# Packed small operands, a new order of the first loads and an earlier split of the first input weights in a two-block transformer kernel

## The chip, the core and the metric

One core of a Trainium2 chip runs the whole program. The metric is the device time of one execution in microseconds; three runs of the kernel before have a median of 1456.27 us (1455.43 to 1457.64). The engines are named as in the profile: PE (TensorE matmul), PEld (its weight load), DVE (VectorE), ACT (ScalarE), POOL (GpSimd) and SP (SyncE, which here issues the DMAs; its queue is SPq).

## What is computed

A batch of one sequence of 256 tokens, width 1024, float32, passes through two blocks. The part that matters here is the first:

```python
mod = jax.nn.silu(c) @ w_ada[l] + b_ada[l]            # 1024 x 6144
sh1, sc1, gt1, sh2, sc2, gt2 = jnp.split(mod, 6, axis=-1)
h = modulate(rmsnorm(x, g_norm1[l]), sh1, sc1)
y = hybrid_mixer(h, w_in[l], ...)
x = x + gt1[:, None, :] * y
h = modulate(rmsnorm(x, g_norm2[l]), sh2, sc2)
y = hierarchical_moe(h, w_rg, b_rg, w_re, b_re, w_e_gate, w_e_up, w_e_down)   # 32 experts, 2 per token
x = x + gt2[:, None, :] * y
# hybrid_mixer
z = h @ w_in
glu_a, glu_b, q, k, v, o, i_pre, f_pre, g_a, g_b = jnp.split(z, offs, axis=-1)
u = jax.nn.silu(layernorm(causal_dwconv(glu_a * sigmoid(glu_b), conv_dw_w, conv_dw_b), ...))
y_a = u @ w_conv_out
hm = mlstm_chunkwise(q, k, v, i_g, f_g)               # 4 heads, then a norm per head, times sigmoid(o)
y_b = hm @ w_m_out
merged = sigmoid(g_a) * y_a + sigmoid(g_b) * y_b
```

The second block has two layers, each with a modulation of the same kind (`ada_w_2`), attention and a gated feed-forward part.

## The kernel before, in words

**Weights.** `load` (L65) takes one of 8 buffers `raw` of 1 MB and has SP issue one DMA into it; there are some 400 MB of weights, so this stream runs through the whole program. A weight that meets a matrix is split in two float32r halves: ACT copies it into `hi`, DVE subtracts to get `lo` (`split` L92, `split_cols` L108 and L110), and `mm3` issues three matmuls (L119 to L121: lo by Hh, hi by Hl, hi by Hh). The activations are split in the same way into `Hh` and `Hl`.

**The modulation.** `mod` is made from `w_ada` in groups of steps (`ada_steps`): each step loads one 1 MB slab and issues 4 matmuls of fp32 into one bank `ada` (the profile counts 8 for the 4); the second step of a block's group first adds the bias by 4 more. The last copies the bank to `adarow` (ACT, L227). Then a use step follows: `ada_cols` (4 matmuls `adac`) and `mod_cols` (DVE, tile `AB`), or `ada_gate`, which splits `adarow` (`gtmp`; ACT copy, DVE subtraction L115), spreads it with 4 matmuls `adag` and copies the two banks to `gate`. The first group (`ada0`, eight steps and a use step) runs at the start; the other three groups of the block stand in the list `queue`, and `fill()` takes the next step from it, one after each input slab, so that their loads and matmuls lie between the others. `fill(len(queue))` before the output products of the mixer takes what is left, and then the steps of the second block's first layer (`cc2`, `ada_w_2`) are appended.

**The start.** SP issues `cs` (constants, 435 KB), small vectors into rows of `vrow`, then the eight slabs of `w_ada` with up to three small loads of the list `late` behind each, x behind the fourth, the second part of the constants `ca`, the gate weights `wif`, the biases `bif` and `brt`, the router weights `wr`, and only then the first slab of `w_in`. Three PE transposes turn `vrow` and `wdr` into columns (`vct`, `wdct`), which DVE and ACT read. x is normed and transposed into four banks `nt` (two halves of the columns by two halves of the tokens), `norm_post` applies the modulation (ACT L344 and DVE L342, tile `gtmp`) and splits the result into `Hh` (L351) and `Hl` (L115). Then `first()` takes each slab of `w_in`: split, 48 matmuls, `fill()`. Four slabs give `glua`, `glub`, `glua`, `glub`, then come the slabs of q and k, the gates, v, the mLSTM in four steps (`pS`, `pw`, `num`), `ga` and `gb`; the normed `hm` is transposed (`hmT`) in between.

**The layer norm of the convolution.** DVE runs the convolution beside the matmuls (`uacc`, L621 and L624). At its end come 4 matmuls `lnm` (mean), ACT's copy, DVE's subtraction (L633), ACT's square (L635), 4 matmuls `lnv`, ACT's root (L640), DVE's reciprocal (L641) and product (L642). The output products `yb` (from `hmT`) and `ya` (from `uacc`) follow.

The order on each engine is set by the tile framework from this program text; an engine runs its instructions in that order.

Of the kernel before, what the change touches and what calls it, by code (L numbers as in the profile page):

```python
# [7 lines left out]
F32 = mybir.dt.float32  # L8
# [3 lines left out]
AF = mybir.ActivationFunctionType  # L12
# [6 lines left out]
KT = 8  # L19
# [9 lines left out]
C_P = 870  # L29
# [8 lines left out]
V_C, V_C2, V_GN1, V_CB, V_LG, V_LB, V_QB, V_GN2 = 0, 8, 16, 24, 28, 32, 36, 44  # L38
V_N1, V_N2, V_MG, V_SG, V_QW, V_LAM, V_END = 52, 68, 84, 88, 89, 121, 125


@with_exitstack
def kernel(ctx: ExitStack, tc: tile.TileContext, I, cst, out):
# [12 lines left out]
    def pb(name):  # L56
        return psum.tile([128, 512], F32, name=name, tag="pb", bufs=3)
# [14 lines left out]
    def load_k(w, k0, k, n0, n):  # L72
        return load(w[k0 * 128:(k0 + k) * 128, n0:n0 + n].rearrange("(k p) n -> p k n", p=128), k, n)
# [54 lines left out]
    early = pha.enter_context(tc.tile_pool(name="early", bufs=1))  # L128
    vrow = early.tile([128, 128], F32, name="vrow")
    x = act.tile([128, 2, D], F32, name="x")  # L130
    wdr = early.tile([124, 128], F32, name="wdr")
    bif = const.tile([8, 1], F32, name="bif")
    brt = const.tile([128, 36], F32, name="brt")
    wr = const.tile([128, KT, 36], F32, name="wr")

    POOL.memset(vrow, 0.0)

    def vload(nm, off, n):
        SP.dma_start(out=vrow[off:off + n], in_=I[nm].rearrange("o (n p) -> (o n) p", p=128))
# [3 lines left out]
    vload("c_2", V_C2, 8)
    vload("g_norm1", V_GN1, 8)
    def lload(i, nm):
        SP.dma_start(out=vrow[V_LAM + i:V_LAM + i + 1, 0:64], in_=I[nm])

    late = [lambda: ada_bias(0, I["b_ada"][0]),
            lambda: vload("conv_dw_b", V_CB, 4), lambda: vload("conv_ln_g", V_LG, 4),
            lambda: vload("conv_ln_b", V_LB, 4), lambda: vload("qk_conv_b", V_QB, 8),  # L150
            lambda: vload("g_norm2", V_GN2, 8), lambda: vload("norm1_g_2", V_N1, 16),
            lambda: vload("norm2_g_2", V_N2, 16), lambda: vload("m_norm_g", V_MG, 4),
            lambda: vload("a_subln_g_2", V_SG, 1),
            lambda: lload(0, "a_lam_q1_2"), lambda: lload(1, "a_lam_k1_2"),
            lambda: lload(2, "a_lam_q2_2"), lambda: lload(3, "a_lam_k2_2"),
            lambda: SP.dma_start(out=vrow[V_QW:V_QW + 32], in_=I["qk_conv_w"].rearrange("o w (n p) -> (o w n) p", p=128)),
            lambda: SP.dma_start(out=wdr, in_=I["conv_dw_w"].rearrange("o w (n p) -> (o w n) p", p=128))]

# [15 lines left out]
    selrr = const.tile([128, 128], F32R, name="selrr")  # L174
    DVE.tensor_copy(selrr, selr)
    half = const.tile([128, 1], F32, name="half")
    POOL.memset(half, -0.5)

    vc = const.tile([128, V_END], F32, name="vc")
    pt = pb("vct")  # L180
    PE.transpose(pt[:, 0:8], vrow[0:8], ident[0:8, 0:8])
    cc = const.tile([128, 8], F32, name="cc")
    ACT.activation(cc, pt[:, 0:8], AF.Silu)
    cc2 = const.tile([128, 8], F32, name="cc2")

# [213 lines left out]
    pt = pb("vct")
    PE.transpose(pt[:, 0:V_END], vrow[0:V_END], ident[0:V_END, 0:V_END])  # L400
    DVE.tensor_copy(vc, pt[:, 0:V_END])
    ACT.activation(cc2, vc[:, V_C2:V_C2 + 8], AF.Silu)
# [18 lines left out]
    wif = pp.tile([128, KT, 8], F32, name="wif")
    SP.dma_start(out=wif, in_=I["w_in"][0][:, 3072:3080].rearrange("(k p) n -> p k n", p=128))
    SP.dma_start(out=brt[:, 0:4], in_=I["b_rg"].to_broadcast([128, 4]))
    SP.dma_start(out=brt[:, 4:36], in_=I["b_re"].to_broadcast([128, 32]))
    SP.dma_start(out=wr[:, :, 0:4], in_=I["w_rg"][0].rearrange("(k p) n -> p k n", p=128))
# [4 lines left out]
    wdc = pp.tile([128, 124], F32, name="wdc")  # L430
    pt = pb("wdct")
    PE.transpose(pt[:, 0:124], wdr, ident[0:124, 0:124])
    DVE.tensor_copy(wdc, pt[:, 0:124])


# [926 lines left out]
def _constants():  # L1362
# [27 lines left out]
    def ang(pos, half, theta):  # L1390
# [39 lines left out]
```

## Time and profile before

| | us |
|---|---|
| median of three runs | 1456.27 |
| the profiled execution's own time | 1455.63 |
| its span, first to last instruction | 1453.9 |
| PE busy in the span | 1303.4 (90%) |
| DVE busy | 620.3 (43%) |
| ACT busy | 490.9 (34%) |

In the rows further down a time is counted from the start of the span. A row of the chain of waits has a start, a duration and what ran (for a DMA, the time in which it was awaited). A row of the timeline has a start, a busy time, engine, line, operation, output and inputs, and the number of instructions merged; square brackets give the idle time before it and what ended it. A row of the windows gives for each engine busy time and instructions, then PE's granted clock as a share of full speed, the busy share of the DMA engines and GB/s.

### The profile page before, as it was taken

How to read it: one execution, taken by the hardware profiler on the slowest of the kernel's cores; microseconds unless marked ns; L12 is line 12 of the kernel's file. 1: busy time of each engine (PE TensorE's matmuls, PEld its weight loads, DVE VectorE, ACT ScalarE, POOL GpSimd, SP SyncE). 2: the span in 40 equal slices, each digit the busy share in tenths (PEclk: the TensorE clock that was granted, in tenths of full speed). 3: DMA queues.
4: the chain of work that ended last, by engine and by line, in shares of the span. 5: the costliest groups of instructions: out<-in, count | busy, mean ns of one | idle time of the engine just before them, and what ended most of it. 6: DMA issues, size and time to landing. Idle time of an engine off the chain costs nothing.

```text
span 1453.9 us, 20075 instructions
## 1 busy us (share of the span) xinstructions
PE 1303.4 (90%) x8125; PEld 888.7 (61%) x8125; DVE 620.3 (43%) x1074; ACT 490.9 (34%) x840; POOL 57.9 (4%) x99
## 2 busy tenths in 40 slices
PE   5799999897997787777778999999999999999997
PEld 1686797634342222121125877698999777799997
DVE  0798856511111011010016545754544765744454
ACT  1465354311010000010006555543443554643442
POOL 0000000000000000000002211000000120000000
PEclk9899999798999899898999999999999999999999
DMA  8987557899999999999999766658555566755500
GB/s 303 401 290 260 197 185 257 310 409 360 392 409 410 414 406 414 410 411 414 408 390 337 257 229 207 244 187 290 174 175 173 203 216 212 285 188 184 174 30 30
DMA packets 200002, 408.83 MB, mean 281 GB/s; under 512 B 10057, under 2 KB 90430, under 8 KB 193762
## 3 DMA queue, kind: packets, MB, share of 16 engines
q1 hardware_dynamic: 199906, 407.51, 76.1%
q8 instruction: 65, 1.06, 0.3%
q14 instruction: 31, 0.25, 0.0%
HBM read 406.43 MB, written 1.05 MB: 280 GB/s over the span
## 4 chain that ended last, share of the span: by engine, by line
PE 74%; DMA 15%; DVE 4%; SPq 3%; issue 2%; ACT 2%; POOL 1%; POOLq 0%; DVEq 0%; ACTq 0%
PE ada L124 5%; DMA raw<-in_w_e_up_dram 5%; PE pu L124 5%; PE pd L124 4%; DMA raw<-in_w_e_down_dram 4%; PE pg L124 4%; PE fu L119 3%; PE fg L120 3%; PE fg L119 3%; PE fg L121 3%; PE fu L120 3%; PE fu L121 3%; PE facc L119 3%; DMA raw<-in_w_e_gate_dram 3%; SPq L69 3%; PE facc L120 3%
## 5 line engine op out<-in xcount | busy, mean ns | idle before, releaser
L92 DVE TENSOR_TENSOR lo<-raw,hi 128x1024 fp32r<-128x1024 f32 x120 | 145.2, 1230 | 126.3 <-ACT hi L90 124.6
L110 DVE TENSOR_TENSOR lo<-raw,hi 128x1024 fp32r<-128x1024 f32 x120 | 146.1, 1224 | 97.0 <-ACT hi L108 96.8
L90 ACT ACTIVATE hi<-raw 128x1024 fp32r<-128x1024 f32 x120 | 125.0, 1061 | 143.9 <-PE facc L121 79.2
L108 ACT ACTIVATE hi<-raw 128x1024 fp32r<-128x1024 f32 x120 | 125.8, 1057 | 123.6 <-issue 55.8
L124 PE MATMUL pu<-raw,xg 128*32 128x512 f32 (+1 forms) x512 | 130.2, 744 | 31.3 <-DMA raw<-in_w_e_up_dram 31.3
L124 PE MATMUL pd<-raw,hT 128*32 128x512 f32 (+1 forms) x512 | 111.1, 597 | 16.7 <-DMA raw<-in_w_e_down_dram 8.8
L124 PE MATMUL pg<-raw,xg 128*32 128x512 f32 (+1 forms) x512 | 109.6, 622 | 17.4 <-DMA raw<-in_w_e_gate_dram 17.4
L926 DVE TENSOR_TENSOR hid<-hid,pu 128x256 f32<-128x256 f32 x20 | 7.5, 418 | 241.9 <-PE pu L124 241.9
L119 PE MATMUL fg<-Hh,lo 128*128 128x256 f32 x352 | 100.7, 286 | 4.3 <-DVE Hh L351 4.3
L124 PE MATMUL ada<-raw,cc 128*32 128x512 f32 x576 | 98.0, 635 | 6.5 <-DMA raw<-in_w_ada_dram 6.5
L124 PEld LDWEIGHTS pu<-raw,xg 128*32 128x32 f32 (+1 forms) x512 | 30.3, 138 | 117.4 <-DMA raw<-in_w_e_up_dram 63.2
L120 PE MATMUL fg<-Hl,hi 128*128 128x256 f32 x352 | 100.4, 285 | 0.9 <-DVE Hl L115 0.9
L119 PE MATMUL fu<-Hh,lo 128*128 128x256 f32 x352 | 100.8, 286 | 0.0
L121 PE MATMUL fg<-Hh,hi 128*128 128x256 f32 x352 | 100.3, 285 | 0.0
L120 PE MATMUL fu<-Hl,hi 128*128 128x256 f32 x352 | 100.3, 285 | 0.0
L121 PE MATMUL fu<-Hh,hi 128*128 128x256 f32 x352 | 100.2, 285 | 0.0
L119 PE MATMUL dense<-hi,Hl 128*128 128x256 f32 x288 | 82.9, 288 | 0.1
L124 PEld LDWEIGHTS pd<-raw,hT 128*32 128x32 f32 (+1 forms) x512 | 30.3, 116 | 84.5 <-issue 58.0
L120 PE MATMUL dense<-lo,Hh 128*128 128x256 f32 x288 | 81.5, 283 | 0.0
L121 PE MATMUL dense<-hi,Hh 128*128 128x256 f32 x288 | 81.4, 284 | 0.0
L124 PEld LDWEIGHTS pg<-raw,xg 128*32 128x32 f32 (+1 forms) x512 | 26.6, 120 | 77.6 <-issue 41.4
L119 PEld LDWEIGHTS fg<-Hh,lo 128*128 128x128 f32 x352 | 68.2, 194 | 6.5 <-issue 4.7
(413 smaller groups left out, 2608.6 us busy)
## 6 DMA issues: line engine op xcount, KB each, us to landing
raw<-in_w_e_gate_dram SPq DMA_DIRECT2D x64, 1024.0 KB
raw<-in_w_e_up_dram SPq DMA_DIRECT2D x64, 1024.0 KB
raw<-in_w_e_down_dram SPq DMA_DIRECT2D x64, 1024.0 KB
raw<-in_ada_w_dram SPq DMA_DIRECT2D x48, 1024.0 KB
raw<-in_f_w_in_dram SPq DMA_DIRECT2D x44, 1024.0 KB
raw<-in_w_ada_dram SPq DMA_DIRECT2D x24, 1024.0 KB
raw<-in_f_w_out_dram SPq DMA_DIRECT2D x22, 1024.0 KB
raw<-in_w_in_dram SPq DMA_DIRECT2D x20, 1024.0 KB
```

The costliest lines, as they stand in the source:

```text
L69: pools.get("dma", SP).dma_start(out=v, in_=src)
L90: ACT.activation(hv, src, AF.Copy)
L92: DVE.tensor_tensor(lv, src, hv.bitcast(F32), ALU.subtract)
L108: ACT.activation(hv, src, AF.Copy)
L110: DVE.tensor_tensor(lv, src, hv.bitcast(F32), ALU.subtract)
L119: PE.matmul(o, al, bh, start=first, stop=False, skip_group_check=True)
L120: PE.matmul(o, ah, bl, start=False, stop=False, skip_group_check=True)
L121: PE.matmul(o, ah, bh, start=False, stop=last, skip_group_check=True)
L124: return PE.matmul(o, a, b, start=first, stop=last, skip_group_check=True)
L926: DVE.tensor_tensor(hid[:, c], hid[:, c], pgu[1][:, c], ALU.mult)
```

## The change

The host packs 13 kinds of small vectors into one array `vectors` [128 x 125] (64 KB) that is loaded as `vc` in the layout in which it is used; `ca`, the convolution's weights, the gates' weights and their bias into `small` [128 x 957] (490 KB, `pk`); and the router's weights and biases into `router` [128 x 324] (166 KB, `rout`). The small loads, the memset of `vrow`, the three transposes and the copies behind them go. The first loads now are: `vc`, a slab of `w_ada`, `cs`, the bias, x, the other seven slabs of `w_ada`, the first slab of `w_in`, `pk`, `rout`, four more slabs of `w_in`, and from there `w_ada` and `w_in` by turns. The first slab of `w_in` is split (`ahead`) in a place of the program before the use step of the modulation; the order of the two middle `nt` banks is exchanged; and the first four slabs take nothing from `queue` (`fills` is 0).

```diff
-    vload("c", V_C, 8)
-    SP.dma_start(out=cs, in_=cst[:, :C_P])
...
-    late = [lambda: ada_bias(0, I["b_ada"][0]),
-            lambda: vload("conv_dw_b", V_CB, 4), lambda: vload("conv_ln_g", V_LG, 4),
...
+    vc = const.tile([128, V_END], F32, name="vc")
+    rout = const.tile([128, R_END], F32, name="rout")
+    wr = rout[:, 0:R_B].rearrange("p (k n) -> p k n", n=36)
+    brt = rout[:, R_B:R_END]
+    SP.dma_start(out=vc, in_=I["vectors"])
...
-    pt = pb("vct")
-    PE.transpose(pt[:, 0:8], vrow[0:8], ident[0:8, 0:8])
-    ACT.activation(cc, pt[:, 0:8], AF.Silu)
+    ACT.activation(cc, vc[:, V_C:V_C + 8], AF.Silu)
+    ACT.activation(cc2, vc[:, V_C2:V_C2 + 8], AF.Silu)
...
-    def first(H, w, n0, name):
-        wt = split_cols(load_k(w, 0, KT, n0, 256))
+    ahead = []
+
+    def first(H, w, n0, name, fills=1):
+        wt = ahead.pop(0) if ahead else split_cols(load_k(w, 0, KT, n0, 256))
...
-        fill()
+        fill(fills)
...
-    for i, f in enumerate(start[:-2]):
-        f()
-        if i == 3:
-            SP.dma_start(out=x, in_=I["x"].rearrange("o (t p) d -> p (o t) d", p=128))
-        for _ in range(3):
-            if late:
-                late.pop(0)()
...
-    for f in start[-2:]:
+    start[0]()
+    SP.dma_start(out=cs, in_=cst[:, :C_P])
+    DVE.tensor_copy(selrr, selr)
+    ada_bias(0, I["b_ada"][0])
+    SP.dma_start(out=x, in_=I["x"].rearrange("o (t p) d -> p (o t) d", p=128))
+    for f in start[1:-1]:
         f()
...
+    ahead.append(split_cols(load_k(I["w_in"][0], 0, KT, 0, 256)))
+    start[-1]()
+    nt[1:3] = nt[2:0:-1]
...
-    SP.dma_start(out=ca, in_=cst[:, C_P:C_PA])
-    SP.dma_start(out=bif, in_=I["b_if"].rearrange("o n -> n o"))
...
-    SP.dma_start(out=wr[:, :, 4:36], in_=I["w_re"][0].rearrange("(k p) n -> p k n", p=128))
+    pk = pp.tile([128, S_END], F32, name="pk")
+    SP.dma_start(out=pk, in_=I["small"])
+    ca, wdc, bif = pk[:, 0:S_W], pk[:, S_W:S_I], pk[0:8, S_B:S_END]
...
+    SP.dma_start(out=rout, in_=I["router"])
     for i in range(2):
-        psa = first(H, w_in, 256 * i, "glua")
-        psb = first(H, w_in, 512 + 256 * i, "glub")
+        psa = first(H, w_in, 256 * i, "glua", 0)
+        psb = first(H, w_in, 512 + 256 * i, "glub", 0)
```

DVE's order at the start, before, from the second `Hl` on (`lo` is the small half of a weight slab, two of them to a slab):

```order
L115 TENSOR_TENSOR Hl<-gtmp,Hh 128x4x128
L342 TENSOR_SCALAR gtmp<-nt,AB_0_192 128x128
L351 CAST Hh<-gtmp 128x4x128
L342 TENSOR_SCALAR gtmp<-nt,AB_0_192 128x128
L115 TENSOR_TENSOR Hl<-gtmp,Hh 128x4x128
L342 TENSOR_SCALAR gtmp<-nt,AB_0_192 128x128 x2
L115 TENSOR_TENSOR wifl<-wif,wifh 128x64
L351 CAST Hh<-gtmp 128x4x128
L110 TENSOR_TENSOR lo<-raw,hi 128x1024
L115 TENSOR_TENSOR Hl<-gtmp,Hh 128x4x128
```

The first `lo` stands behind the fourth `Hh`. Now, from the tile `AB` on:

```order
L117 TENSOR_TENSOR lo<-raw,hi 128x1024 x2
L332 CAST Hh<-gtmp 128x4x128
L518 CAST sel4r<-pk 4x512
L122 TENSOR_TENSOR Hl<-gtmp,Hh 128x4x128
L332 CAST Hh<-gtmp 128x4x128
L122 TENSOR_TENSOR wifl<-pk,wifh 128x64
L122 TENSOR_TENSOR Hl<-gtmp,Hh 128x4x128
L522 CAST maskr<-pk 128x128
L323 TENSOR_SCALAR gtmp<-nt,AB_0_217 128x128 x2
L332 CAST Hh<-gtmp 128x4x128
L323 TENSOR_SCALAR gtmp<-nt,AB_0_217 128x128
L122 TENSOR_TENSOR Hl<-gtmp,Hh 128x4x128
```

Both halves of the first slab now stand ahead of the first `Hh`; behind these rows come `gtmp`, a `lo` of the second slab, the fourth `Hh`, the other `lo`, the fourth `Hl`. ACT has the two `hi` copies behind its third `gtmp` of twelve, where they stood behind all of them. On PE the first 12 matmuls need the first two `Hh` and `Hl`, the next ones the second slab's `lo`, and the last of the first 26 the fourth `Hl`.

PE's order around the convolution's layer norm, before (the piece with `adag` lies among the products `gb`, well ahead of `lnm`; of the `yb` rows between `lnm` and `lnv`, 28 in all, one stands):

```order
L121 MATMUL gb<-Hh,hi 128x256
L124 MATMUL adag<-gtmp,selrr 128x512 x4
L119 MATMUL gb<-Hh,lo 128x256
...
L124 MATMUL lnm<-uacc,ones 128x256 x4
L119 MATMUL yb<-bhl,lo 128x256
...
L124 MATMUL lnv<-sq,ones 128x256 x4
L120 MATMUL yb<-bhl,hi 128x256
```

`lnm` and `lnv` lie among `yb` matmuls, and `adag` (the gate gt2) is done long before. Now:

```order
L128 MATMUL gb<-Hh,hi 128x256
L131 MATMUL ada<-raw,cc 32x512 x4
L131 MATMUL lnm<-uacc,ones 128x256 x4
L131 MATMUL ada<-raw,cc_89 32x512 x4
L131 MATMUL ada<-bias,cs 32x512 x4
L131 MATMUL ada<-raw,cc_89 32x512 x3
L131 MATMUL lnv<-sq,ones 128x256 x4
L131 MATMUL ada<-raw,cc_89 32x512 x9
L131 MATMUL adag<-gtmp,selrr 128x512 x4
L126 MATMUL yb<-bhl,lo 128x256
```

All `yb` stand behind `adag`; between `lnm`, `lnv` and `adag` there are only steps of the second block's modulation. `adag` waits for DVE's subtraction `gtmp<-adarow,gtmp`, and that now stands on DVE directly behind the reciprocal and the product of the layer norm, whose buffer of `gtmp` it also takes over.

PE's order from the last `num` to `hmT`, before (41 rows of `ga` in the first gap, 40 in the second):

```order
L124 MATMUL num<-va,wT 128x129 x3
L120 MATMUL ga<-Hl,hi 128x256
...
L124 MATMUL ada<-raw,cc 32x512 x3
...
L603 MATMUL hmT<-cs,hm 128x128 x4
```

Now there are 40 and 26:

```order
L131 MATMUL num<-va,wT 128x129 x3
...
L131 MATMUL ada<-bias,cs 32x512 x2
L131 MATMUL ada<-raw,cc 32x512 x4
...
L574 MATMUL hmT<-cs,hm 128x128 x4
```

So 15 matmuls `ga` that lay ahead of `hmT` now lie behind it, and three more of `ada` lie ahead.

## Rows read from the trace of the kernel before

**Rows 1.** Chain of waits, 0 to 70 us, in order of time: start, duration, what

```profile
0.74 3.43 DMA cs<-constants_dram
...
21.82 10.69 DMA raw<-in_w_ada_dram
32.55 1.11 PE ada L124 x8
...
35.69 2.91 ACT gtmp L344 x8
...
43.78 0.58 PE glua L119
...
46.71 0.21 PE glua L119
...
47.46 0.12 PE glua L121
...
51.07 0.99 PE ada L124 x8
```

**Rows 2.** Windows: engines' busy time, PEclk, DMA share, GB/s

```profile
0.00:10.00 10.00, 1.32 (x9) 0.41 (x9) 0.54 (x4) 1.46 (x2) 0.94 (x11) 1.00 0.73 238
10.00:20.00 10.00, 8.26 (x38) 0.80 (x32) 0.00 (x0) 0.00 (x0) 0.00 (x0) 1.00 0.98 370
28.00:30.00 2.00, 2.00 (x11) 1.86 (x9) 0.57 (x4) 0.21 (x1) 0.00 (x0) 0.53 1.01 427
32.00:34.00 2.00, 1.06 (x8) 0.16 (x8) 0.53 (x2) 0.32 (x1) 0.00 (x0) 1.00 0.49 44
300.00:740.00 440.00, 349.99 (x1710) 117.29 (x1710) 46.78 (x103) 34.80 (x70) 0.00 (x0) 0.92 1.03 405
```

**Rows 3.** Timeline of SP, 24 to 26 us

```profile
25.15 4.96 SPq L423 DMA_DIRECT2D brt<-in_b_rg_dram  x1
```

**Rows 4.** Waits of PE, 43.7 to 266 us: total us, times, longest

```profile
PE glua L119 <- DVE lo L110: 8.2, 1, 8.2
PE hmT L603 <- DVE hm L595: 0.6, 1, 0.6
```

**Rows 5.** Timeline of PE, two early stretches

```profile
15.67 1.94 PE L124 MATMUL ada<-raw,cc 128*32 128x512 f32 x8 [1.08 <-DMA raw<-in_w_ada_dram]
...
72.36 1.06 PE L124 MATMUL ada<-raw,cc 128*32 128x512 f32 x8
```

**Rows 6.** Timeline of DVE and ACT at the start

```profile
39.09 0.69 DVE L115 TENSOR_TENSOR Hl<-gtmp,Hh 128x512 fp32r<-128x512 f32 x1
...
42.17 0.43 DVE L351 CAST Hh<-gtmp 128x512 fp32r<-128x512 f32 x1
...
40.99 2.00 ACT L108 ACTIVATE hi<-raw 128x1024 fp32r<-128x1024 f32 x2 [0.86 <-DMA raw<-in_w_in_dram]
```

**Rows 7.** Timeline of PE, ACT and DVE around the layer norm

```profile
204.64 1.89 PE L124 MATMUL lnm<-uacc,ones 128*128 128x256 f32 x8
206.19 0.47 PE L119 MATMUL yb<-bhl,lo 128*128 128x256 f32 x1
...
209.94 1.99 PE L124 MATMUL lnv<-sq,ones 128*128 128x256 f32 x8
211.58 0.47 PE L120 MATMUL yb<-bhl,hi 128*128 128x256 f32 x1
...
206.42 1.23 DVE L92 TENSOR_TENSOR lo<-raw,hi 128x1024 fp32r<-128x1024 f32 x1 [2.06 <-ACT hi L90]
...
211.97 0.48 ACT L640 ACTIVATE gtmp<-lnv,eps 128x256 f32<-128x256 f32 x1 [0.78 <-PE lnv L124]
...
212.48 1.75 DVE L641 RECIPROCAL gtmp<-gtmp 128x256 f32<-128x256 f32 x1 [2.41 <-ACT gtmp L640]
...
214.90 1.22 DVE L642 TENSOR_TENSOR uacc<-uacc,gtmp 128x1024 f32<-128x1024 f32 x1
...
183.40 0.68 DVE L115 TENSOR_TENSOR gtmp<-adarow,gtmp 128x512 fp32r<-128x512 f32 x1
```

More of the change, by code (lines that the diff above doesn't have):

```diff
@@ L39 @@
 V_N1, V_N2, V_MG, V_SG, V_QW, V_LAM, V_END = 52, 68, 84, 88, 89, 121, 125
+S_W = C_PA - C_P
+S_I = S_W + 124
+S_B = S_I + 64
+S_END = S_B + 1
+R_B = KT * 36
+R_END = R_B + 36
 @with_exitstack
@@ L128 @@
     early = pha.enter_context(tc.tile_pool(name="early", bufs=1))
-    vrow = early.tile([128, 128], F32, name="vrow")
     x = act.tile([128, 2, D], F32, name="x")
[L131 to L139, printed above, removed]
-    vload("c", V_C, 8)
-    SP.dma_start(out=cs, in_=cst[:, :C_P])
[L143 to L146, printed above, removed]
-    late = [lambda: ada_bias(0, I["b_ada"][0]),
-            lambda: vload("conv_dw_b", V_CB, 4), lambda: vload("conv_ln_g", V_LG, 4),
[L150 to L157, printed above, removed]
+    vc = const.tile([128, V_END], F32, name="vc")
[3 more added lines that the diff above has]
+    SP.dma_start(out=vc, in_=I["vectors"])
     ident = cs[:, C_ID:C_ID + 128]
@@ L174 @@
     selrr = const.tile([128, 128], F32R, name="selrr")
-    DVE.tensor_copy(selrr, selr)
     half = const.tile([128, 1], F32, name="half")
     POOL.memset(half, -0.5)
-    vc = const.tile([128, V_END], F32, name="vc")
-    pt = pb("vct")
-    PE.transpose(pt[:, 0:8], vrow[0:8], ident[0:8, 0:8])
     cc = const.tile([128, 8], F32, name="cc")
-    ACT.activation(cc, pt[:, 0:8], AF.Silu)
+    ACT.activation(cc, vc[:, V_C:V_C + 8], AF.Silu)
     cc2 = const.tile([128, 8], F32, name="cc2")
+    ACT.activation(cc2, vc[:, V_C2:V_C2 + 8], AF.Silu)
     bias_t = {}
@@ L391 @@
     start = ada0(0, I["w_ada"][0], cc, lambda: vc[:, V_GN1:V_GN1 + 8])
-    for i, f in enumerate(start[:-2]):
-        f()
-        if i == 3:
-            SP.dma_start(out=x, in_=I["x"].rearrange("o (t p) d -> p (o t) d", p=128))
-        for _ in range(3):
-            if late:
-                late.pop(0)()
[L399 to L402, printed above, removed]
-    for f in start[-2:]:
+    start[0]()
[4 more added lines that the diff above has]
+    for f in start[1:-1]:
         f()
@@ L416 @@
     w_in = I["w_in"][0]
-    ca = pp.tile([128, C_PA - C_P], F32, name="ca")
-    SP.dma_start(out=ca, in_=cst[:, C_P:C_PA])
-    SP.dma_start(out=bif, in_=I["b_if"].rearrange("o n -> n o"))
[L421 to L425, printed above, removed]
-    SP.dma_start(out=wr[:, :, 4:36], in_=I["w_re"][0].rearrange("(k p) n -> p k n", p=128))
+    pk = pp.tile([128, S_END], F32, name="pk")
+    SP.dma_start(out=pk, in_=I["small"])
+    ca, wdc, bif = pk[:, 0:S_W], pk[:, S_W:S_I], pk[0:8, S_B:S_END]
+    wif = pk[:, S_I:S_B].rearrange("p (k n) -> p k n", n=8)
     u_le = ca[:, C_LE - C_P:C_LE - C_P + 128]
@@ L429 @@
     sel4 = ca[0:4, C_SEL4 - C_P:C_SEL4 - C_P + 512].rearrange("p (h m) -> p h m", h=4)
[L430 to L433, printed above, removed]
     ifg = pp.tile([128, 2, 8], F32, name="ifg")
@@ L1401, in _constants, with _packed, tiled @@
     return c
+def _packed(inputs, c):
+    import numpy as np
+    rows = np.zeros((V_END, 128), np.float32)
+    for at, name in ((V_C, "c"), (V_C2, "c_2"), (V_GN1, "g_norm1"), (V_CB, "conv_dw_b"), (V_LG, "conv_ln_g"),
+                     (V_LB, "conv_ln_b"), (V_QB, "qk_conv_b"), (V_GN2, "g_norm2"), (V_N1, "norm1_g_2"),
+                     (V_N2, "norm2_g_2"), (V_MG, "m_norm_g"), (V_SG, "a_subln_g_2"), (V_QW, "qk_conv_w")):
+        a = np.asarray(inputs[name]).reshape(-1, 128)
+        rows[at:at + a.shape[0]] = a
+    for i, name in enumerate(("a_lam_q1_2", "a_lam_k1_2", "a_lam_q2_2", "a_lam_k2_2")):
+        rows[V_LAM + i, 0:64] = np.asarray(inputs[name]).reshape(64)
+    def tiled(a):
+        a = np.asarray(a)
+        return a.reshape(KT, 128, -1).transpose(1, 0, 2)
+    router = np.zeros((128, R_END), np.float32)
+    router[:, 0:R_B] = np.concatenate([tiled(inputs["w_rg"][0]), tiled(inputs["w_re"][0])], axis=2).reshape(128, R_B)
+    router[:, R_B:R_B + 4] = np.asarray(inputs["b_rg"]).reshape(1, 4)
+    router[:, R_B + 4:R_END] = np.asarray(inputs["b_re"]).reshape(1, 32)
+    small = np.zeros((128, S_END), np.float32)
+    small[:, 0:S_W] = c[:, C_P:C_PA]
+    small[:, S_W:S_I] = np.asarray(inputs["conv_dw_w"]).reshape(124, 128).T
+    small[:, S_I:S_B] = tiled(np.asarray(inputs["w_in"])[0][:, 3072:3080]).reshape(128, 64)
+    small[0:8, S_B] = np.asarray(inputs["b_if"]).reshape(8)
+    return {"vectors": np.ascontiguousarray(rows.T), "router": router, "small": small}
 _INS = ["x", "c", "w_ada", "b_ada", "g_norm1", "w_in", "b_if", "conv_dw_w", "conv_dw_b", "conv_ln_g", "conv_ln_b",
@@ L1423 @@
     arrays["constants_dram"] = _constants()
+    for name, a in _packed(inputs, arrays["constants_dram"]).items():
+        arrays[f"{name}_dram"] = a
+        aps[name] = nc.dram_tensor(f"{name}_dram", a.shape, F32, kind="ExternalInput").ap()
     cst = nc.dram_tensor("constants_dram", (128, C_END), F32, kind="ExternalInput").ap()
```

## The prediction, made before the changed kernel was timed

> **What bounds the kernel now.** I read the waits of PE first, then the chain of waits at the start, then the windows, and last the timelines of the three places that the change touches. The waits say that from 43.7 us to 266 us, the whole of the mixer, PE waits for two things only: 8.2 us for its first weights and 0.6 us at `hmT` [rows 4]. So in that part PE is the bound, and a microsecond saved or lost on PE is one of the mixer's end. Behind it the experts are bound by the loads: 405 GB/s at a DMA share of 1.03 from 300 to 740 us [rows 2]. Their weights start to flow when the mixer lets go of its buffers, so a mixer that ends earlier shifts the rest by as much, and I carry every microsecond through one to one.
>
> The chain at the start shows why PE begins at 43.78: the last modulation weights are waited for until 32.55, the modulation starts at 35.69 (the first row of `gtmp`), and the first matmul `glua` follows 8.1 us later [rows 1]. The windows show that the loads are not at their rate there: 238 GB/s in the first 10 us and 370 in the next, against 427 at 28 to 30 us, and a hole of 44 GB/s at 32 to 34 [rows 2]. The hole is SP's: one issue of the router's bias took it 4.96 us [rows 3], and the first slab of `w_in` stands behind it.
>
> **The change part by part.** A measurement of this kernel can tell about 0.2%, 2.9 us, from no change.
>
> *A, the loads up to the last modulation weights.* Now the stream is eight slabs and x at 1.049 MB each, `cs` 0.445, `vc` 0.064 and the bias 0.025: 9.97 MB, in large pieces, with up to eight in flight, so that SP's issue times lie beside the transfers. The start-up is what the wait for `cs` holds beyond its bytes: 3.43 - 0.445/0.405 = 2.3 us, from 0.74 on [rows 1]. At the experts' 405 GB/s [rows 2] the last slab is there at 0.74 + 2.3 + 24.6 = 27.65 in place of 32.55: **-4.9 us**. Bounds: with 370 GB/s 30.0 (-2.55), with 427 GB/s 26.4 (-6.15) [rows 2]. I take 405, as it holds over 440 us of the same slabs. [...]
>
> *B, from there to the modulation.* It takes 35.69 - 32.55 = 3.14 us now [rows 1], its last step at full speed (1.11). Steps that came with gaps between them took 1.94 [rows 5], and with slabs that come every 2.6 us each step has such a gap: **+0.9** for a last step at the slower pace; bounds 0 and +1.9 (the 4 `adac` slower as well).
>
> *C, the first products.* From the modulation's start the first matmul takes 8.1 us [rows 1]. In the new order DVE has both `lo` ahead of the first `Hh`, and ACT both `hi` behind its third `gtmp`. I add the durations in that order, with `gtmp` 0.36 (2.91 for 8) [rows 1], two `hi` 2.0, `Hh` 0.43, `Hl` 0.69 [rows 6] and `lo` 1.23 [rows 7]: first `Hh` at 4.9, second `Hl` at 7.1, the second slab's first `lo` at 10.8, the fourth `Hl` at 13.0. So PE starts a microsecond earlier but has 12 matmuls only until 10.8, and 26 done at 13.6. Before, at 13.6 us (49.3 on the clock) it had done 16 at 0.21 and from 47.1 on some 19 at 0.12 [rows 1], together 35. Nine matmuls behind at 0.12: **+1.0**. Bounds: -1.0 if the earlier start counts alone, +2.0 if the clock stays low through the second gap. That w_in's first slab itself comes early is worth nothing more: its `hi` now waits 0.86 for it [rows 6], and that wait is off the path once DVE's order decides.
>
> *D, the five groups of steps moved out of the first four slabs.* The four fills (steps and bias) cost 0.99 per 4 matmuls [rows 1], and they cost the same later, on a PE that is never idle: 0 in sum. But the order moves behind them, and two places lose their cover. *D1, the layer norm.* Before, `yb` matmuls lie between `lnm`, `lnv` and what follows. Now 11 matmuls of steps (2.7 us at 0.99 for four) lie between `lnm` and `lnv`, where the chain over ACT and DVE took 209.94 - 206.19 = 3.75 us [rows 7], a part of it behind a `lo` on DVE that ended at 207.65; without that some 3.15, so about 0.45 idle (1.0 at most). Then `adag` waits for a subtraction that stands behind the reciprocal and the product: from the end of `lnv` (211.58) the reciprocal's end at 214.23 is 2.65 us, and 1.22 + 0.68 more make 4.55 [rows 7], while PE has 9 matmuls, 2.2 us. About 2.35 idle, with `yb`, ready for long, queued behind `adag`. Together **+2.8**; bounds 2.0 (all durations overlapping at their ends) and 4.3 (the next 16 matmuls at 0.21 in place of 0.12, as at 43.78). The `yb` work itself is not lost, and `ya` has it as cover afterwards. *D2, `hmT`.* Its chain over DVE and POOL is as before and already ends 0.6 us late [rows 4]. 15 matmuls `ga` at 0.12 fewer lie ahead (1.75) and three of `ada` more (0.75): **+1.0**; bounds 0 and 1.75.
>
> *At nothing:* the memset, three transposes and copies that go stood in gaps in which PE waited for slabs (1.08 idle ahead of a step [rows 5]); without that cover they would be under 1 us. The order of the banks only serves C. `pk` and `rout`, 0.66 MB behind the first slab of `w_in`, delay the second slab by 1.6 us; DVE's order asks for it only at about 8 us behind the modulation. Should that cover fail, it would cost up to those 1.6.
>
> **Sum:** -4.9 + 0.9 + 1.0 + 2.8 + 1.0 = +0.8, on the profiled execution's 1455.63 (span 1453.9): 1456.4. The median of the runs is 0.64 higher than that execution, which is below what a run can tell; I forecast **1456.5**, no change: what the start gains, two waits later give back.
>
> **The rivals.**
> 1. *The start gains more than I reckon, and it shows.* Loads at 427 GB/s (-6.15), the last step at full speed (B 0), the earlier first matmul counting (C -1.0), with D as above: -3.35, **1452.3**. For it: 427 was seen in the same stretch [rows 2], and the step at 32.55 did run at full speed behind a gap [rows 1]. Against: the early steps at 1.94 [rows 5], and DVE's order, which is fixed.
> 2. *The load queue does not get faster:* the early rate is the transfers' own and not the small loads', so it stays at 370 GB/s. That is also the case in which the packing does not do what it says. A is -2.55 and the sum +3.15: **1458.8**. For it: the DMA share was 0.98 in that stretch already [rows 2]. Against: 427 and 405 elsewhere.
> 3. *The waits cost the clock too.* PE at its half speed after an idle stretch did its first 16 matmuls in 0.21 in place of 0.12 [rows 1], 1.5 us. If the gaps at `adag` and `hmT` each bring that, it is 3.0 more: +3.8, **1459.4**, slower. It decides as soon as more than 2.1 us come on top of the sum, that is when both places lose it. For it: early gaps of 1 us already go with steps at 1.94 [rows 5]. Against: the gaps are 1.6 and 2.4 us, not 8.2, with PE busy on both sides.
>
> **How the numbers follow.** The forecast 0.47 (nearly all of it within 2.9 us of before), the first rival 0.28 (faster), the second 0.10 and the third 0.15 (slower). The range goes from a little below the first rival, 1451.6, to the third, 1459.8; outside are a start at all its best bounds, and D1 and D2 at all their worst. Of the forecast's own case 1454 to 1459 would be the range. Faster by over 0.2% 0.28, within 0.47, slower 0.25.
>
> **What would show it.** In the changed profile: the last wait for `w_ada` ends at about 27.6, at 400 GB/s and more from 3 us on with no hole (A); the modulation starts near 31.7 (B); a first `glua` near 39, with a second wait of `glub` for `lo` of the second slab (C); waits of PE at `adag` near 2.4 and `lnv` near 0.5 (D1), and at `hmT` near 1.6 (D2). Experts that begin to load within 1 us of before would be the sum. I am wrong if `adag` does not wait, if the rate stays at 370, or if the mixer's end moves by more than the waits named here.

## The result and the profile after

The changed kernel takes **1476.88 us** (median of 4 runs, 1475.73 to 1479.35) against 1456.19 for the kernel before on the same chip: a ratio of 1.0137, 95% interval [1.0124, 1.0150], 20.7 us slower, far outside the forecast's range of 1451.6 to 1459.8. The profiled execution has a span of 1474.4 us, 20.5 more than before.

Where the time lies is seen first in the page's row of GB/s, in 40 equal slices of the span (36.9 us each; 36.3 before). The page before:

```profile
span 1453.9 us, 20075 instructions
...
GB/s 303 401 290 260 197 185 257 310 409 360 392 409 410 414 406 414 410 411 414 408 390 337 257 229 207 244 187 290 174 175 173 203 216 212 285 188 184 174 30 30
```

The page after:

```profile
span 1474.4 us, 20022 instructions
...
PE 1305.2 (89%) x8122; PEld 891.2 (60%) x8122; DVE 620.2 (42%) x1072; ACT 491.0 (33%) x840; POOL 57.9 (4%) x98
...
GB/s 368 322 236 247 236 307 172 334 393 326 390 393 393 399 387 399 388 398 394 392 398 332 295 204 209 217 255 260 194 181 172 197 187 214 276 201 195 174 30 30
...
DMA packets 196505, 408.84 MB, mean 277 GB/s; under 512 B 6676, under 2 KB 86932, under 8 KB 190264
```

PE, DVE, ACT and POOL are busy as long as before, within 2 us. From the ninth slice to the twenty-first, the experts, the loads run at 387 to 399 GB/s in most slices where they ran at 406 to 414. The first two slices together moved about as much (368 and 322 for 303 and 401), more of it in the first, as forecast.

The windows say the same for the stretches of [rows 2] and for the middle of the experts (engines' busy time, then PEclk, DMA share and GB/s):

```profile
0.00:10.00 10.00, 3.58 (x16) 0.43 (x16) 0.82 (x7) 1.59 (x3) 0.80 (x10) 1.00 0.80 296
10.00:20.00 10.00, 7.41 (x40) 3.08 (x40) 1.18 (x3) 3.93 (x9) 1.10 (x2) 1.00 1.01 421
32.00:34.00 2.00, 0.34 (x2) 0.25 (x2) 0.24 (x2) 1.35 (x4) 0.00 (x0) 0.50 1.06 343
300.00:740.00 440.00, 337.95 (x1652) 114.97 (x1648) 46.77 (x103) 34.06 (x68) 0.00 (x0) 0.92 1.02 388
400.00:700.00 300.00, 225.50 (x1138) 70.44 (x1137) 29.17 (x70) 22.42 (x44) 0.00 (x0) 0.91 1.04 394
```

and before, for the last of them:

```profile
400.00:700.00 300.00, 234.26 (x1179) 70.64 (x1179) 29.20 (x67) 23.61 (x46) 0.00 (x0) 0.92 1.04 411
```

The start answers the prediction: 296 GB/s for 238, 421 for 370, and the hole of 44 is gone. Over 300 to 740 us there are 388 in place of 405, at the same DMA share of 1.02 to 1.03: the DMA engines are as busy as before, and their packets take longer. In the records of single packets from 400 to 700 us, the rows of 2 KB took 84.4 ns in the mean before and 88.3 after, those of 4 KB 159.2 and 163.7.

Two issues of SP mark the stages: `gf` goes out when the mixer is done, `rot` when the experts let go of their tiles. The timeline of SP before, and after:

```profile
261.25 0.34 SPq L986 DMA_DIRECT2D gf<-in_g_final_dram  x1
...
763.10 0.34 SPq L1004 DMA_DIRECT2D rot<-constants_dram  x1
```

```profile
260.17 0.34 SPq L957 DMA_DIRECT2D gf<-in_g_final_dram  x1
...
782.98 0.34 SPq L975 DMA_DIRECT2D rot<-constants_dram  x1
```

Up to `gf` the changed kernel is 1.1 us ahead; between the two marks it loses 21.0 us (522.8 for 501.9); behind `rot` 0.6 (691.4 for 690.8). So the whole loss arises in the experts, of whose code the change touches no line (only the router's weights and biases come from another tile).

In the mixer the waits of PE from 35 to 266 us are these, where [rows 4] had two:

```profile
PE glua L126 <- DVE Hh L332: 6.5, 1, 6.5
PE adag L131 <- DVE gtmp L122: 1.7, 1, 1.7
PE hmT L574 <- DVE hm L566: 1.3, 1, 1.3
...
PE glub L126 <- DVE lo L117: 0.7, 1, 0.7
```

And in the experts the timeline of PE shows, behind the branch that guards the rarely used way for crowded experts, a second stop. Before there is one of 6.95 us, then `gath` (the products that gather the tokens of an expert) runs through:

```profile
351.42 0.55 PE L124 MATMUL gath<-gr,xl 128*128 128x256 f32 x1 [6.95 <-DMA raw<-in_w_e_gate_dram]
351.77 0.41 PE L124 MATMUL gath<-gr,xh 128*128 128x256 f32 x1
```

After there are two, the second behind two matmuls of one product, in which the profile shows nothing that PE waits for ("issue"):

```profile
350.13 0.55 PE L131 MATMUL gath<-gr,xl 128*128 128x256 f32 x1 [6.67 <-issue]
350.48 0.41 PE L131 MATMUL gath<-gr,xh 128*128 128x256 f32 x1
355.93 0.37 PE L131 MATMUL gath<-gr,xl 128*128 128x256 f32 x1 [5.03 <-issue]
```

### The profile page after: what moved, and what is told of

It is laid out like the page before. It is cut to its first block, busy times and chain, and to the rows that moved or that the text cites. A ratio compares the mean times of both kernels' runs of the same rounds, so it can differ in the third digit from the quotient of the medians.

```text
span 1474.4 us, 20022 instructions
## 1 busy us (share of the span) xinstructions
PE 1305.2 (89%) x8122; PEld 891.2 (60%) x8122; DVE 620.2 (42%) x1072; ACT 491.0 (33%) x840; POOL 57.9 (4%) x98
## 3 DMA queue, kind: packets, MB, share of 16 engines
HBM read 406.43 MB, written 1.05 MB: 276 GB/s over the span
## 4 chain that ended last, share of the span: by engine, by line
PE 53%; DMA 14%; SPq 3%; DVE 2%; issue 2%; ACT 1%; POOL 0%; POOLq 0%; DVEq 0%; ACTq 0%
DMA raw<-in_w_e_up_dram 8%; DMA raw<-in_w_e_down_dram 4%; PE ada L131 3%; PE pu L131 3%; PE fg L127 3%; PE fu L126 3%; PE pd L131 3%; PE fg L126 3%; PE fg L128 3%; PE fu L127 3%; PE fu L128 3%; PE facc L126 3%; SPq L76 3%; PE pg L131 3%; PE facc L127 2%; PE facc L128 2%
## 5 line engine op out<-in xcount | busy, mean ns | idle before, releaser
L131 PE MATMUL pg<-raw,xg 128*32 128x512 f32 (+1 forms) x512 | 112.6, 651 | 21.0 <-DMA raw<-in_w_e_gate_dram 20.8
L896 ACT ACTIVATE hid<-pg 128x256 f32<-128x256 f32 x20 | 6.6, 381 | 203.2 <-PE pg L131 203.2
```

What stands on the lines that cost most here:

```text
L131: return PE.matmul(o, a, b, start=first, stop=last, skip_group_check=True)
L896: ACT.activation(hid[:, c], pgu[0][:, c], AF.Silu)
```

## The experiments

**What slows the experts' loads.** The tiles of a kernel lie behind one another in SBUF. The change replaced some tiles of the first pool by another (`rout`, 1296 bytes per partition, for `wr`, `brt` and `bif`, together 1300; as placed in the two programs, where each of these tiles starts at a multiple of 32, 1312 for 1344), and the pool became 32 bytes per partition shorter. The eight load buffers behind it start at 25568 bytes of their partition, where they started at 25600. Theory S: this start address sets the rate. Rival H: the three new arrays shift the weights in HBM, or the new order does it.

Run a32 pads the first pool of the changed kernel:

```diff
+    pad = const.tile([128, 8], F32, name="pad")
+    nc.gpsimd.memset(pad, 0.0)
     cs = const.tile([128, C_P], F32, name="cs")
```

> The changed kernel with an unused tile of 32 bytes per partition in the first pool. Its constants' pool is 32 bytes shorter than before, so that the eight load buffers start at 25568 bytes of their partition, an odd multiple of 32, where they started at 25600. This run puts them back at 25600 and leaves the three new arrays in HBM. Theory S (the start address of the load buffers in SBUF sets the rate of the loads): 300 to 740 us at about 410 GB/s as before, in place of some 393, and 1454 to 1459 us, 18 to 22 less than the changed kernel. Rival H (the new arrays shift the weights in HBM, or the mixer's new order costs the rate later): 393 GB/s and 1475 to 1479 us as the changed kernel.

1460.65 us, ratio to before 1.0028 [1.0016, 1.0041], and the rate is back:

```profile
400.00:700.00 300.00, 234.37 (x1190) 73.50 (x1189) 29.21 (x70) 22.42 (x44) 0.00 (x0) 0.92 1.04 411
```

S holds and H falls: the arrays and the order are still those of the change. The time is 1.7 us above what S allowed; what is left, 4 us, is the subject of the second part. Between the marks a32 takes 505.6 us (`gf` at 262.18, `rot` at 767.77) for the changed kernel's 522.8: the padding alone gives back 17.2 of the 21.0. The same with 16 elements in place of 8 (64 bytes):

> The changed kernel with 64 bytes of padding: buffers at 25632, again an odd multiple of 32. Control for the padding itself. Theory S: about 393 GB/s and 1475 to 1479 us, as the changed kernel. A theory in which any padding helps (tiles that share a line, another conflict of neighbours): 1454 to 1459 us. Rival H: 1475 to 1479 us, so this run alone does not tell S from H.

1477.89 us, 394 GB/s: padding as such does not help. With 24 elements (96 bytes):

> The changed kernel with 96 bytes of padding: buffers at 25664, a multiple of 64 but not of 128 or 256. If theory S holds with a unit of 64 bytes: 410 GB/s and 1454 to 1459 us. If the unit is 128, 256 or more (each row of a transfer then begins in the middle of a unit): 393 GB/s or a rate between, 1465 to 1479 us.

1477.91 us, 393 GB/s. A start at a multiple of 64 is not enough. The kernel before with 8 elements of padding:

> The kernel before with 32 bytes of padding: buffers at 25632 in place of 25600, nothing else changed. Theory S: the experts' loads fall from 410 to about 393 GB/s and the time rises by 18 to 23 us, to 1474 to 1479. Rival H: 1456 us as before.

1473.84 us, 1.0130 [1.0098, 1.0162], and

```profile
400.00:700.00 300.00, 224.60 (x1126) 68.34 (x1126) 26.82 (x62) 22.40 (x44) 0.00 (x0) 0.91 1.04 394
```

So 32 bytes and nothing else make the kernel before slower by 1.3%, 16.9 us. The unit was narrowed on the kernel before, first with 32 elements of padding (128 bytes):

> The kernel before with 128 bytes of padding: the first eight buffers at 25728, a multiple of 128 but not of 256 (the second eight at 163520, 192 past a multiple of 256). Theory S with a unit of 256 bytes: 394 GB/s and 1473 to 1478 us, as with 32 bytes. With a unit of 128 bytes: 411 GB/s and 1456.

1475.95 us, 1.0134 [1.0115, 1.0153], 394 GB/s. Then the pool of small tiles (640 bytes) was put ahead of the buffers, with 128 bytes of padding:

```diff
+    small = ctx.enter_context(tc.tile_pool(name="small", bufs=2))
     rawp = ctx.enter_context(tc.tile_pool(name="raw", bufs=RAW_BUFS))
     act = ctx.enter_context(tc.tile_pool(name="act", bufs=1))
-    small = ctx.enter_context(tc.tile_pool(name="small", bufs=2))
...
+    pad = const.tile([128, 32], F32, name="pad")
```

> The kernel before with the first eight load buffers at 26368, a multiple of 256 but not of 512. Theory S with a unit of 256 bytes: 411 GB/s and 1455 to 1458 us. With a unit of 512 bytes or more: 394 GB/s and 1473 to 1478. The second eight stand at 163520, off either unit, as in the kernel before.

1457.0 us, 0.9992 [0.9981, 1.0003], 411 GB/s. Of the units tried (32, 64, 128, 256 and 512 bytes) it is 256. The paddings moved other tiles too, so two runs changed the order of the pools only, iso:

```diff
-    rawp = ctx.enter_context(tc.tile_pool(name="raw", bufs=RAW_BUFS))
     act = ctx.enter_context(tc.tile_pool(name="act", bufs=1))
     small = ctx.enter_context(tc.tile_pool(name="small", bufs=2))
+    rawp = ctx.enter_context(tc.tile_pool(name="raw", bufs=RAW_BUFS))
```

> The kernel before with its first pools in another order (the load buffers behind the tiles of x and the small ones), which puts the eight load buffers at 59008, 128 past a multiple of 512, while every other tile keeps its place relative to 512. Theory S (it is the load buffers' own start): 394 GB/s and 1473 to 1478 us. Rival T (another tile that the paddings shifted too, such as x or the experts' activations, slows the loads): 411 GB/s and 1455 to 1458.

1476.44 us, 1.0138 [1.0112, 1.0165], 394 GB/s. And iso2, with `raw` between `act` and `small`:

> Control of the run named iso: the same tiles in an order that leaves the load buffers at 58368, a multiple of 512. Theory S: 411 GB/s and 1455 to 1458 us. If the place of the buffers among the others counts and not their start: 394 GB/s and 1473 to 1478.

1457.37 us, 0.9999 [0.9987, 1.0011], 411 GB/s. It is the buffers' own start.

The experts' stage has 16 buffers; the second eight, which take every other load, start 64 past a multiple of 256 in the kernel before. If each buffer counts, there was more to gain. Run m192:

```diff
+        gap = pp.tile([128, 48], F32, name="gap")
+        nc.gpsimd.memset(gap, 0.0)
         km = pp.tile([128, C_END - C_KB], F32, name="km")
```

> The kernel before with 192 bytes of padding in the experts' pool. Of the 16 load buffers of the experts' stage, eight start at 25600 (a multiple of 256) and the other eight at 163392, which is 64 bytes past a multiple of 256; the padding puts the second eight at 163584, a multiple of 256 as well. The runs so far gave 394 GB/s with all 16 off a multiple of 256 and 411 with eight of them on it, and in the start, where only the first eight are used, 424 to 428 at 10 to 20 us. Theory S with a unit of 256 bytes: the experts' loads rise to about 425 GB/s at 400 to 700 us and the kernel before gets 12 to 18 us faster, 1439 to 1445. If the second eight buffers do not count (the unit is larger than 256, or something else sets the rate): 411 GB/s and 1456.

1458.13 us, 1.0003 [0.9992, 1.0014], 412 GB/s: nothing gained, my expectation failed. Perhaps their unit was larger, so m512 put their pools ahead of the experts' other tiles, behind 384 bytes:

```diff
-    with tc.tile_pool(name="moe", bufs=1) as pp, \
-            tc.tile_pool(name="raw2", bufs=3) as raw2, tc.tile_pool(name="raw3", bufs=5) as raw3:
+    with tc.tile_pool(name="gap", bufs=1) as gap, tc.tile_pool(name="raw2", bufs=3) as raw2, \
+            tc.tile_pool(name="raw3", bufs=5) as raw3, tc.tile_pool(name="moe", bufs=1) as pp:
+        nc.gpsimd.memset(gap.tile([128, 96], F32, name="gap"), 0.0)
```

> The kernel before with the second eight load buffers of the experts' stage at 124928, a multiple of 512 (163392 before, 64 past one; 163584, 256 past one, gave 412 GB/s). Theory S with a unit of 512 bytes: all 16 buffers are on it now, so the experts' loads rise from 411 to 425 to 428 GB/s and the kernel gets 10 to 18 us faster, 1439 to 1447. If the second eight do not count: 411 GB/s and 1455 to 1458.

1459.55 us, 1.0020 [1.0003, 1.0037], 412 GB/s: not that either. Two runs asked whether the second eight count at all. r2off is m192 with 8 elements in place of 48:

> The kernel before with 32 bytes of padding in the experts' pool: the first eight load buffers stay at 25600 (a multiple of 256), the second eight move from 163392 (64 past one) to 163424 (96 past one, an odd multiple of 32). If the second eight do not count at all: 411 GB/s and 1455 to 1458 us. If they need a multiple of 64 only: 394 to 403 GB/s and 1464 to 1476. If both eights count alike and what holds the rate at 411 is another limit: 411 too, so this run and the next are read together.

1455.56 us, 0.9991 [0.9981, 1.0000], 411 GB/s. r2on is iso with the 48 elements of m192:

> The run named iso (first eight at 59008, 128 past a multiple of 512, 394 GB/s) with the second eight at 163584, a multiple of 256, where iso has them 64 past one. If the second eight do not count: 394 GB/s and 1474 to 1478 us. If both eights count alike, and half of the buffers on a multiple of 256 are enough to reach the other limit of 411: 411 GB/s and 1455 to 1458. Between, 400 to 405 GB/s: each half counts for itself.

1457.02 us, 1.0003 [0.9989, 1.0017], and

```profile
400.00:700.00 300.00, 226.15 (x1183) 71.45 (x1181) 30.01 (x71) 22.97 (x45) 0.00 (x0) 0.95 1.04 411
```

So the second eight do count: with the first eight off (as in iso, 394) a right start of the second alone gives 411. Either half on a multiple of 256 is enough, both give no more (412), neither gives 394.

The records of single packets say more. From 400 to 700 us, in every run with at least one half on a multiple of 256, the middle 80% of the 2 KB packets took 84 ns each, so those into the half that is off are no slower. With both halves off they spread from 84 to 95 ns. A wrong start thus cost a packet time only where all loads had one. The difference is 4 to 6 ns whatever the size: 84.4 to 88.3 ns in the mean for 2 KB, 159.2 to 163.7 for 4 KB (before and after), and at the start, where the slabs have rows of 8 KB, 309.1 to 314.8 (a32 and after, 10 to 27 us). That is 5%, 3% and 2%, so short rows lose most. At 411 GB/s the DMA share is 1.04, and the packets take the shortest times seen, 84 and 159 ns. Why these are the shortest, and why one half suffices, these runs do not tell.

**What is left of the change.** The second stop at `gath` was tried with the padded kernel and six idle transposes (run pe6), which make PE's program longer ahead of the branch:

```diff
     ada_bias(0, I["b_ada"][0])
+    pt = pb("spare")
+    for i in range(6):
+        nc.tensor.transpose(pt[:, 0:128], cs[:, 128:256], ident)
     SP.dma_start(out=x, in_=I["x"].rearrange("o (t p) d -> p (o t) d", p=128))
```

> The changed kernel with the 32 bytes of padding (load buffers at 25600) and six idle PE transposes in the start, which stand where PE waits for slabs. The program of PE is shorter by some ten instructions since the change; in the padded kernel PE stops twice at its first two pieces of `gath` behind the branch of the fallback, 6.6 us and then 4.5 us after only two matmuls, while before it stops once (7.0). [...] Rival (the second stop comes of the experts' loads, which lie otherwise against the routing): it stays at 4 to 5 us, and the time at 1459 to 1462.

1457.85 us, 1.0004 [0.9990, 1.0018], 2.8 less than a32 (run on another chip), where I expected the second stop to go and 4 to 5 less; `gath` runs through behind the first stop:

```profile
351.97 0.55 PE L131 MATMUL gath<-gr,xl 128*128 128x256 f32 x1 [6.53 <-issue]
352.31 0.42 PE L131 MATMUL gath<-gr,xh 128*128 128x256 f32 x1
352.53 0.42 PE L131 MATMUL gath<-gr,xl 128*128 128x256 f32 x1
```

From the first `gath` to `rot` it takes 412.2 us in place of 415.8 in a32 (before: 411.7). Up to `gf` the two traces agree within 0.1 us (262.27 for 262.18), and between the marks pe6 takes 501.9 us, as the kernel before (501.9), for 505.6 in a32. So the stop goes with the length of the program ahead. The run noahead further down, whose program for PE is one instruction shorter than a32's (7065 for 7066), agrees: its second stop comes behind three matmuls in place of two.

```profile
345.50 0.41 PE L131 MATMUL gath<-gr,xl 128*128 128x256 f32 x1
350.43 0.58 PE L131 MATMUL gath<-gr,xh 128*128 128x256 f32 x1 [4.51 <-issue]
```

The packets' records show transfers near both stops. On the queue that the profile calls "instruction" a packet of 16 KB lands 1.5 to 1.6 us before the end of the first stop in all 20 traces, and another 1.2 to 1.4 us before the end of the second stop in each of the six that have one (in the changed kernel at 354.59, PE goes on at 355.93). In the kernel before such a packet lands at 355.57, and PE runs on without a stop. What these packets hold, and whether PE waits for them, no run shows. PE's programs of 7065 and 7066 instructions have the second stop; those of 7072 (pe6) and 7077 (the kernel before) have not.

Run fills, the padded kernel with the fills given back:

```diff
-        psa = first(H, w_in, 256 * i, "glua", 0)
-        psb = first(H, w_in, 512 + 256 * i, "glub", 0)
+        psa = first(H, w_in, 256 * i, "glua")
+        psb = first(H, w_in, 512 + 256 * i, "glub")
```

> The padded kernel with the fills of the first four slabs given back (each takes a step of the queue again), all else of the change kept. Prediction's terms D1 and D2: the waits at `adag` (1.7 us) and the larger one at `hmT` go, the low clock behind `adag` too, and the mixer ends 2 to 4 us earlier: 1456.5 to 1459 against the padded 1460.7. If the fills only move the steps (the waits are hidden elsewhere): 1460 to 1461.5.

1459.9 us, 1.0030 [1.0016, 1.0045]. The waits at `adag` are gone and `hmT` is at 0.5; `gf` is issued at 259.12 for 262.18, 3.1 earlier, within what was expected. But the median, above the 1456.5 to 1459 expected, is only 0.8 below a32, which the intervals do not tell from nothing. `gf` is read from one execution of each; in those of the kernel before and of its variants, whose mixer is unchanged, it lies anywhere from 259.5 to 262.7 (m512 aside, where it is issued elsewhere).

Run noahead, the padded kernel without the early split and the exchange of the banks:

```diff
-    ahead.append(split_cols(load_k(I["w_in"][0], 0, KT, 0, 256)))
     start[-1]()
-    nt[1:3] = nt[2:0:-1]
```

> The padded kernel without the early split of the first slab and with the old order of the `nt` banks; the fills stay at 0. Prediction's term C: the early split puts PE behind by about 1 us over the first four slabs, so without it 1459 to 1460. If the early split helps instead (first matmul earlier by as much as PE waits): 1461 to 1463. Within 0.6 us of 1460.7: it is worth nothing either way.

1456.79 us, 1.0003 [0.9993, 1.0012], 3.9 below a32 where 1 to 2 were expected, still with the second stop. The first four slabs are done at 63.10 in place of 66.16. PE's first `glua` is 0.5 later (38.91 for 38.37), but it then runs through, and its clock rises earlier. Windows of a32, then of noahead:

```profile
35.00:48.00 13.00, 8.68 (x38) 8.13 (x39) 9.61 (x19) 5.55 (x13) 0.00 (x0) 0.51 1.07 401
```

```profile
35.00:48.00 13.00, 9.09 (x63) 9.09 (x64) 9.79 (x15) 6.50 (x8) 0.00 (x0) 0.71 1.08 401
```

38 matmuls at a granted clock of 0.51 against 63 at 0.71. Of the 3.1 us, 0.9 lie ahead of the split products: the last step of the modulation took 1.06 in noahead's execution for 1.94 in a32's, and the modulation starts at 31.30 for 32.22. From there to the end of the first four slabs it takes 31.8 in place of 33.9, so the early split and the exchange together cost some 2 us. In the profiled executions `gf` is 6.2 earlier (256.03); the other 3 lie in stretches of low clock later in the mixer (a32 has 0.83 at 130 to 140 us, noahead 1.00, and the changed kernel 1.00 too) and are not put down to the split.

Run loads keeps the packing, the padding, the order of the loads and the six transposes, and takes back the early split, the exchange and the zero fills (the edits of pe6, fills and noahead together):

> Packing and the new order of the loads alone: load buffers at 25600, the six PE transposes, fills as before, no early split. The prediction's A and B alone are -4.0 us: 1452 to 1453.5, below the kernel before. If the start's gain is not carried through the mixer or the experts (their routing, their branch): 1455 to 1457.

**1453.33 us, 0.9976 [0.9964, 0.9987]**, faster than the kernel before by 3.5 us, within the expected range: the start's gain comes through once the rest is undone. Run best adds the 48 elements of m192:

> The packing and the new order of the loads (load buffers at 25600, six idle transposes, fills as before, no early split), and the second eight buffers at 163584. Theory S: the gains add, 1453.3 - 12 to 18 = 1435 to 1441. If the experts' stage is then bound by PE or the routing: 1441 to 1448.

1450.64 us, 0.9959 [0.9943, 0.9974], above both expected ranges; the expected gain of the second eight is not there, as in m192, and the interval overlaps that of loads. Run best2 is best with the fills at 0:

> As the run named best, but with the fills of the first four slabs at 0, as in the change. Prediction's terms D1 and D2 (the waits at `adag` and `hmT`): 1 to 3 us slower than best. If the start without fills gives it back: the same within 1 us.

1452.33 us, 0.9964 [0.9951, 0.9977], not to be told from best. The waits at `adag` (1.7) and `hmT` (1.3) are back in its trace, yet its mixer is no longer: from the modulation's start to `gf` it takes 224.5 us, and 225.3 in best; noahead takes 224.7, loads 225.6. Only beside the early split is there a difference, 230.0 in a32 for 226.9 in fills.

## Why the prediction was wrong

**The step that failed** is in the part on what bounds the kernel: "a mixer that ends earlier shifts the rest by as much, and I carry every microsecond through one to one". It took the experts' 405 GB/s [rows 2] as a property of the stage, and the sum has no term for the place of the load buffers. The rate hung on where these buffers start, and the change moved them by 32 bytes: 394 for 411 GB/s from 400 to 700 us. Of the 21.0 us lost between the marks `gf` and `rot`, 17.2 come back with the padding (a32). The other 3.7 come back with six idle transposes (pe6): these are the second failed step, in the part "At nothing", which priced the three transposes by their work and not by their place in PE's program. With both undone the experts take what they took before, 501.9 us.

The sizes were in front of me: `rout` is named in the change, and tiles of a pool lie behind one another. What such a move costs only the runs show: with the second eight buffers off, starts of the first eight at multiples of 256 give 411 GB/s, at odd multiples of 32, 64 and 128 they give 393 to 394. How far past a multiple of 256 the start lies made no difference in the two cases measured: at the start, where only the first eight buffers are used, rows of 8 KB took 314.8 ns at 224 past it (the changed kernel) and 314.6 at 32 past it (a64), for 309.1 on it (a32).

Up to the mixer's end the sum came out, in part because misses of its terms offset one another:

- *A.* The last slab was forecast at 27.65, at 400 GB/s and more; it came at 27.83, at 421 from 10 to 20 us and 398 from 20 to 30.

```profile
27.83 1.93 PE L131 MATMUL ada<-raw,cc 128*32 128x512 f32 x8 [0.79 <-DMA raw<-in_w_ada_dram]
30.47 1.87 PE L131 MATMUL adac<-cs,adarow 128*128 128x4 f32 x8 [0.70 <-ACT adarow L208]
...
38.80 0.58 PE L126 MATMUL glua<-Hh,lo 128*128 128x256 f32 x1 [6.46 <-DVE Hh L332]
```

- *B.* Step and `adac` both ran at the slower pace, the dearer end of the range (1.93 and 1.87 for 1.06 and 1.05). The modulation starts at 32.65 where 31.7 was forecast: 4.82 us behind the last wait for 3.14, which is +1.7 for +0.9.

```profile
32.65 1.16 ACT L325 ACTIVATE gtmp<-nt,AB 128x128 f32<-128x128 f32 x3 [2.23 <-DVE AB L239]
```

- *A, B and C together.* The first `glua` was forecast near 39 and came at 38.80. The first four slabs ended at 65.64 against 72.36 - 3.97 = 68.39 [rows 5], without the three steps and the bias that lay between them: -2.75, forecast -3.0. From the modulation's start they take 33.0 us for 32.7 before, so C is +0.3 here (33.9 and +1.2 in a32), forecast +1.0. Against the new order of loads without the early split (noahead, 31.8) it is 1.2 and 2.1: with the stop at `glub` the clock stayed low longer (0.51 for 0.71 from 35 to 48 us, the windows above).
- *D1 and D2.* `adag` waited 1.7 (forecast 2.35), `lnv` not at all (0.45), `hmT` 1.3 (1.6). Low clock followed `adag`, as the third rival has it: after the wait the timeline of PE goes from 0.12 to 0.21 between matmuls, and the window has 0.65. The wait alone does not bring it: in noahead PE waits as long at `adag` (1.7) and goes on at 0.12, at a granted clock of 1.00 from 212 to 220 us. What else it takes is open. Nor did the waits alone make the mixer longer there (see best2 above). From the modulation's start to `gf` the changed kernel takes 2.0 us more than before and a32 4.4, where C and D were to add 4.8.

```profile
205.62 1.99 PE L131 MATMUL lnv<-sq,ones 128*128 128x256 f32 x8
207.55 2.76 PE L131 MATMUL ada<-raw,cc 128*32 128x512 f32 x18
212.03 0.74 PE L131 MATMUL adag<-gtmp,selrr 64*128 64x512 f32 x4 [1.72 <-DVE gtmp L122]
212.70 0.38 PE L126 MATMUL yb<-bhl,lo 128*128 128x256 f32 x1
...
213.72 0.41 PE L126 MATMUL yb<-bhl,lo 128*128 128x256 f32 x1
213.93 0.41 PE L127 MATMUL yb<-bhl,hi 128*128 128x256 f32 x1
```

```profile
212.00:216.00 4.00, 3.98 (x21) 3.61 (x22) 0.00 (x0) 3.99 (x8) 0.00 (x0) 0.65 1.05 413
```

The timeline of noahead at the same place:

```profile
209.34 0.73 PE L131 MATMUL adag<-gtmp,selrr 64*128 64x512 f32 x4 [1.72 <-DVE gtmp L122]
210.00 0.39 PE L126 MATMUL yb<-bhl,lo 128*128 128x256 f32 x1
210.22 0.28 PE L127 MATMUL yb<-bhl,hi 128*128 128x256 f32 x1
210.34 0.28 PE L128 MATMUL yb<-bhl,hi 128*128 128x256 f32 x1
```

- *The sum.* Forecast +0.8 at the mixer's end; measured -1.1 in the changed kernel and +0.9 in a32, one execution each, and the kernel before with its variants spreads as far (259.5 to 262.7). That the sum was near is in part luck.
- *At nothing.* The absence of the three transposes and of other instructions made PE's program shorter (7066 instructions for 7077): 5.0 us at the second stop in the changed kernel, 3.7 us between the marks and 2.8 us of the median (a32 against pe6) once the loads run at their rate.

None of the three rivals was the case. The part behind `rot` takes 691 to 693 us in the runs with the change; the kernel before and its variants (without m512, which issues `rot` earlier) take 689.5 to 692.4, so no loss is shown there.

## What to carry to other kernels

An edit that only exchanges tiles moves every tile behind them: write down where the buffers of the big loads start before and after, and keep them at a multiple of 256 bytes per partition when a stage is bound by loads (here 411 GB/s for 394, and one half of them was enough). Look at the stages that an edit does not touch with the same windows as those that it does. And when a program gets shorter, look behind its branches for a stop with no releaser (here 4.5 to 5.1 us).

## What the runs showed of the hardware

- Eight load buffers at 25600, 26368 or 58368 bytes (multiples of 256): 411 GB/s in the experts; at 25568, 25632, 25664, 25728 or 59008: 393 to 394 GB/s, at the same DMA share of 1.04 (the second eight buffers off a multiple of 256 in all of these). With 16 buffers in turn, one half on a multiple of 256 is enough for 411, both give 412.
- With all buffers off a multiple of 256, packets of 2, 4 and 8 KB took 88.3, 163.7 and 314.8 ns in the mean (the changed kernel), for 84.4, 159.2 and 309.1 with the first eight on it (a32).
- PE stood 6.2 to 7.2 us before its first matmul behind the branch in every run, and a second stop of 4.5 to 5.1 us stood in six of them; with six more instructions of PE's program ahead of it there was none (pe6, for 4.5 in a32). Each stop ended 1.2 to 1.6 us after a 16 KB packet had landed on the instruction queue; in the kernel before such a packet landed at 355.57 without a stop.
- A wait of 1.7 us at `adag` was followed by matmuls at a low granted clock in the changed kernel (0.50 from 213.7 to 216 us) and in a32 (0.71 in the mean from 216 to 220), and by matmuls at 1.00 in noahead (212 to 220).
